# One PSUM bank moved from the recurrences to the projection, the sixth Strassen product in a bank of its own, and a set of reordered steps, in a hybrid mLSTM and SSD layer

## The chip, the core and the metric

The kernel runs on one core of one Trainium2 chip. The metric is device microseconds (us) of that core for one call, the median of several runs. Lower is better. Engines are called PE (matrix multiply), DVE (vector), ACT (scalar), POOL (GpSimd) and SP (the engine that issues every DMA of this kernel, in one in-order queue).

## What is computed

One decoder layer on 2,048 tokens of width 1,024, in float32. `reference.py`, cut to its core:

```python
h = rms_norm(x, norm_w[l])
proj = h @ w_in[l]                                   # 1024 -> 6680 columns
q, k, v, i_pre, f_pre, o_pre, z_m, z_s, xbc, dt_raw = jnp.split(proj, SPLIT_POINTS, axis=-1)
hm = mlstm_chunkwise(q, k, v, log_i, log_f)          # 4 heads, chunks of 128 tokens
hm = hm * lax.rsqrt(jnp.mean(hm * hm, -1, keepdims=True) + EPS) * mlstm_norm_w * sigmoid(o_pre) * silu(z_m)
xs, Bm, Cm = split(silu(causal_depthwise_conv(xbc)))
y = ssd_chunked(xs, softplus(dt_raw + dt_bias), A, Bm, Cm) + d_skip * xs     # 2 groups of 8 heads
y = rms_norm_per_group(y * silu(z_s)) * ssd_norm_w
x = x + concat(hm, y) @ w_out[l]
return rms_norm(x, final_norm_w)
```

## The kernel before

**Stages.** The tokens are taken as two super blocks of 1,024 (stages 0 and 1 of the program); stages 2 and 3 multiply the mixed result by the two halves of `w_out`. Every large product is one level of Strassen's scheme in a form with seven products: a job (`strassen`, L273 to 296) computes a 256 x 1,024 piece of output from seven products of 128 x 512 x 512, and there are 52 + 16 jobs. Float32 accuracy comes from splitting each operand into a high and a low half (`split`, L187; `hi` by ACT, `lo` by DVE): a product is 12 matmuls on 512 columns (L270).

**A pair's seven products** go to three PSUM banks of the pool `psp` (tag `pj`, four banks): `pa` takes L11·R11, then S2·T2, S1·T1 and S4·R22 on top; `ps` takes L12·R21; `pd` takes S3·T3, then L22·T4 on top. Each intermediate sum of `pa` is copied out by ACT (L276, L283, L289, L292) before the next product lands on it, and DVE adds `ps` or `pd` (L280, L290, L296). The order on PE interleaves two jobs: S2, S3, L11 of the next job, S1, L12 of the next job, S4, L22.

**Recurrences** are woven between these products, at most one step after each (`Weave`). `rec_head` (L661) is the mLSTM of one head: 8 chunks, `scores`, `memory`, then `gate` and `turn` some products later; `turn` multiplies the numerator by a diagonal matrix `dg` that holds the norm's factor, which transposes and scales at once (L749). `rec_group` (L774) is the SSD scan of one group: `decay` loads the rows `E` and makes the decay matrix on DVE (L797) and ACT, `tokens` transposes B and x (L812 to 816) and forms `xdt`, `cbm`, `xw` and `E` times `cbm` on DVE, `states` reads the state H (L842) and adds to it (L852, L857, L859), `outs` multiplies by E (L870), `norm` and `spread` follow three and five products later. All their PSUM tiles come from the pool `psr` (tag `rc`, four banks).

**Background work.** `next_h` (L492) normalises and splits the second super block during stage 0 and writes it to memory; its generator has 68 steps, spread over 82 products. `next_w` (L522) does the same for `w_out`. At a change of stage `refill` (L386) loads the 14 tiles of the right operand, one pair per product. `gates_mm` (L541) computes the gates' projection: it loads `wg`, splits it, and its matmuls (L562 to 564) stand on PE right behind the first job's S2 product.

Only PE's order is fixed by hand; the other engines' queues are ordered when the program is built. Each queue runs in order.

Of the kernel before, what the change touches and what calls it, by code (L numbers as in the profile page):

```python
# [69 lines left out]
def hybrid_layer(ctx, tc, x, norm_w, w_in, b_igate, b_fgate, conv_w, conv_b, dt_bias,  # L70
# [8 lines left out]
    psp = ctx.enter_context(tc.tile_pool(name="psp", bufs=4, space=PSUM))  # L79
    psr = ctx.enter_context(tc.tile_pool(name="psr", bufs=4, space=PSUM))  # L80
# [192 lines left out]
    def strassen(L, R, oa, ob, copy):  # L273
# [15 lines left out]
        nc.scalar.copy(ob[1], pa)  # L289
        nc.vector.tensor_add(ob[1], pd, ob[1])  # L290
        yield
        product(pa, L["S4"], R["R22"], False)  # L292
        copy(oa[1], pa)
# [199 lines left out]
    def next_h():  # L493

        for c in range(NCH):
# [3 lines left out]
            for i in range(2):  # L499
# [5 lines left out]
                for _ in range(4):  # L505
                    yield
# [34 lines left out]
    def gates_mm(s, R):  # L541
        wg = r2("wg", 4 * 4 * NG)
# [7 lines left out]
        wh = mk([P, 1024], "t", 1, "wgs", F32R) if s else mk([P, 6, P], "g3", 2, "wgs", F32R).rearrange("p a b -> p (a b)")  # L550
        hi, lo = wh[:, 0:16 * NG], wh[:, 16 * NG:32 * NG]
# [113 lines left out]
    def rec_head(s, h):  # L665
# [38 lines left out]
        def memory(n):  # L704
# [27 lines left out]
            dg = r5("dgm")  # L732
            nc.gpsimd.tensor_scalar_mul(dg, ident, sq)
            L["m", n] = (mx, dg)
# [8 lines left out]
        def turn(n):  # L743
            b, c = seq[n]
            mx, dg = L.pop(("m", n))
            g = L.pop(("gt", n))
            ps = rc_tile()
            for i in range(2):
                nc.tensor.matmul(ps[:, i * P:(i + 1) * P], lhsT=mx[:, i * P:(i + 1) * P], rhs=dg,  # L749
                                 start=True, stop=True)  # L750
# [25 lines left out]
    def rec_group(s, g):  # L776
# [30 lines left out]
        def tokens(n):  # L807
# [7 lines left out]
            for i in range(4):  # L815
                nc.tensor.transpose(xps[:, i * P:(i + 1) * P], t[:, 2 + i, :], ident)
            xdt = r2("xdt")
            nc.vector.tensor_tensor(xdt.rearrange(v3, e=HD), xps.rearrange(v3, e=HD),
                                    bc(G["sp"][:, c, ws], HD), op=ALU.mult)
            bt = r5("bt")  # L820
            nc.scalar.copy(bt, cps[:, P:2 * P])
            cbm = r5("cbm")
            nc.vector.tensor_mul(cbm, cps[:, 0:P], tri)
            xw = r2("xw")
            nc.vector.tensor_tensor(xw.rearrange(v3, e=HD), xps.rearrange(v3, e=HD),
                                    bc(G["dend"][:, c, hs], HD), op=ALU.mult)
# [4 lines left out]
        def states(n):  # L831
# [6 lines left out]
            y = r2("y").rearrange("p (a l) -> p a l", a=4)  # L838
            if H is not None:
# [4 lines left out]
                nc.vector.tensor_mul(y, ops.rearrange("p (a l) -> p a l", a=4), ea)  # L844
                for i in range(4):
                    nc.scalar.activation(ea[:, i, :], t[:, 2 + i, :], AF.Copy, scale=dcol[:, g, i:i + 1])
                nc.vector.tensor_add(y, y, ea)
            else:
                for i in range(4):
                    nc.scalar.activation(y[:, i, :], t[:, 2 + i, :], AF.Copy, scale=dcol[:, g, i:i + 1])  # L850
# [260 lines left out]
```

## Time and profile before

| | |
|---|---|
| median of 3 runs | 1888.11 us (1884.36 to 1892.07) |
| profiled execution, own time | 1880.11 us |
| its span | 1878.4 us |
| PE, DVE, ACT, POOL busy | 1693.1, 1299.4, 899.9, 398.6 us |
| PE granted clock, mean | 0.960 of full speed |
| DMA moved | 405.33 MB |

The profiled execution is 0.4% below the median. PE is busy for 90% of the span, so the end is set by PE's work and by the some 185 us in which it stands still. "Idle before" an instruction, with the engine and the line that it waited for, is therefore the column to read; idle time on the other engines costs nothing by itself.

### The profile page before, as it was taken

To read this page: it belongs to the slowest core of one execution; us is meant where nothing else is said; L and a number is where in the kernel's file an instruction comes from. 1 tells how busy PE (TensorE), PEld (TensorE's weight loads), DVE (VectorE), ACT (ScalarE), POOL (GpSimd) and SP (SyncE) were. 2 spreads that over 40 slices of the span, in tenths; PEclk is the share of its full clock that TensorE was granted. 3 is DMA by queue.
4 is the path that set the end of the run, shared out by engine and by line. 5 is a ranking of instruction groups with operands and counts; after the bars stand their busy time and mean duration, and the time that the engine had idled before them with its cause. 6 is when DMAs were issued, how large, how long until landed. Compare 5 with 4: busy or idle time off the path is not lost.

```text
span 1878.4 us, 25378 instructions
## 1 busy us (share of the span) xinstructions
PE 1693.1 (90%) x8200; PEld 1380.0 (73%) x8200; DVE 1299.4 (69%) x2417; ACT 899.9 (48%) x1912; POOL 398.6 (21%) x597
## 2 busy tenths in 40 slices
PE   5999999899999793998999999989979878997997
PEld 4688887788788681776788878768768667776885
DVE  7677968966657782697685886565668557863775
ACT  5345644465566551343554455555556433432443
POOL 2000303223121220032121231201112134431322
PEclk8999999999999896998999999999989989998999
DMA  5355667578778699364565758888867977578553
GB/s 149 96 166 171 192 197 214 176 244 249 233 210 233 185 308 358 98 198 134 181 181 162 240 176 271 257 285 274 270 195 256 358 264 223 185 254 336 181 161 112
DMA packets 358323, 405.33 MB, mean 216 GB/s; under 512 B 30224, under 2 KB 284432, under 8 KB 352816
## 3 DMA queue, kind: packets, MB, share of 16 engines
q1 hardware_dynamic: 358192, 403.72, 66.7%
q8 instruction: 65, 1.06, 0.2%
q14 instruction: 66, 0.54, 0.1%
HBM read 251.40 MB, written 152.24 MB: 215 GB/s over the span
## 4 chain that ended last, share of the span: by engine, by line
PE 32%; DMA 22%; DVE 12%; issue 5%; ACT 4%; SPq 3%; POOL 2%; DVEq 0%; POOLq 0%; ACTq 0%
PE pj L270 26%; DMA E<-arow 4%; DMA nmi<-mrow 3%; DVE E L797 2%; DMA we<-in_w_out 2%; DVE cd L317 2%; DMA wb<-in_w_in 1%; DMA xr<-in_x 1%; PE rc L852 1%; DMA T4l<-ws1T 1%; DMA mx<-mix 1%; DVE hql L398 1%; DMA z<-gd 1%; PE rc L870 1%; DMA ws1T<-hqh 1%
## 5 line engine op out<-in xcount | busy, mean ns | idle before, releaser
L730 POOL TENSOR_SCALAR sq<-dn,sq 128x1 f32<-128x1 f32 x64 | 50.3, 785 | 663.0 <-ACT sj L728 532.2
L270 PE MATMUL pj<-R22h,S4h 128*128 128x512 f32 x272 | 118.3, 435 | 34.7 <-ACT ob L289 19.1
L270 PE MATMUL pj<-T2h,S2h 128*128 128x512 f32 x272 | 114.9, 423 | 2.3 <-ACT T2h L441 2.3
L270 PE MATMUL pj<-T1l,S1h 128*128 128x512 f32 x272 | 107.9, 397 | 8.8 <-DMA T1l<-ws1T 7.0
L270 PE MATMUL pj<-T1h,S1h 128*128 128x512 f32 x272 | 113.1, 416 | 2.5 <-ACT ob L283 2.4
L270 PE MATMUL pj<-T4h,L22h 128*128 128x512 f32 x272 | 113.3, 416 | 1.9 <-DMA T4h<-ws1T 1.9
L270 PE MATMUL pj<-R11h,L11h 128*128 128x512 f32 x272 | 113.9, 419 | 0.0
L270 PE MATMUL pj<-R21h,L12h 128*128 128x512 f32 x272 | 112.9, 415 | 0.0
L270 PE MATMUL pj<-R22l,S4h 128*128 128x512 f32 x272 | 111.6, 410 | 0.0
L270 PE MATMUL pj<-R22h,S4l 128*128 128x512 f32 x272 | 111.6, 410 | 0.0
L270 PE MATMUL pj<-T2l,S2h 128*128 128x512 f32 x272 | 108.2, 398 | 3.2 <-DMA T2l<-ws0T 1.9
L270 PE MATMUL pj<-T3h,S3h 128*128 128x512 f32 x272 | 109.7, 403 | 0.0
L270 PE MATMUL pj<-T4l,L22h 128*128 128x512 f32 x272 | 106.9, 393 | 1.9 <-DMA T4l<-ws1T 1.9
L270 PE MATMUL pj<-T2h,S2l 128*128 128x512 f32 x272 | 108.0, 397 | 0.0
L270 PE MATMUL pj<-T1h,S1l 128*128 128x512 f32 x272 | 107.6, 396 | 0.0
L270 PE MATMUL pj<-T4h,L22l 128*128 128x512 f32 x272 | 106.9, 393 | 0.0
L270 PE MATMUL pj<-R21l,L12h 128*128 128x512 f32 x272 | 106.5, 392 | 0.0
L270 PE MATMUL pj<-R21h,L12l 128*128 128x512 f32 x272 | 106.5, 391 | 0.0
L270 PE MATMUL pj<-R11h,L11l 128*128 128x512 f32 x272 | 106.3, 391 | 0.0
L270 PE MATMUL pj<-T3l,S3h 128*128 128x512 f32 x272 | 106.1, 390 | 0.2 <-DMA T3l<-ws0T 0.2
L270 PE MATMUL pj<-T3h,S3l 128*128 128x512 f32 x272 | 106.1, 390 | 0.0
L270 PE MATMUL pj<-R11l,L11h 128*128 128x512 f32 x272 | 106.1, 390 | 0.0
(331 smaller groups left out, 4681.4 us busy)
## 6 DMA issues: line engine op xcount, KB each, us to landing
wa<-in_w_in SPq DMA_DIRECT2D x52, 512.0 KB, 5.3
s<-sum SPq DMA_DIRECT2D x52, 512.0 KB, 5.5
hd<-ob SPq DMA_DIRECT2D x32, 512.0 KB, 4.2
E<-arow SPq DMA_DIRECT2D x32, 512.0 KB, 5.4
hin<-hd SPq DMA_DIRECT2D x64, 256.0 KB, 5.6
mx<-mix SPq DMA_DIRECT2D x32, 512.0 KB, 4.4
wb<-in_w_in SPq DMA_DIRECT2D x26, 512.0 KB, 4.8
sum<-ls SPq DMA_DIRECT2D x26, 512.0 KB, 3.8
```

Source lines behind the costliest of these rows:

```text
L270: nc.tensor.matmul(ps, lhsT=l[:, k, :], rhs=r[:, k, :], start=start and k + n == 0, stop=k == 3 and n == 2, skip_group_check=True)
L317: nc.vector.scalar_tensor_tensor(dst, raw[:, q:q + SUP], cw[:, t, q:q + 1], dst, op0=ALU.mult, op1=ALU.add)
L398: nc.vector.tensor_sub(lo, src, hi.bitcast(F32))
L730: nc.gpsimd.tensor_scalar(sq, dn, DV * EPS, sq, op0=ALU.mult, op1=ALU.add)
L797: nc.vector.tensor_scalar(E[:, r, :], E[:, r, :], G["cum"][:, c, k:k + 1], 0.0, op0=ALU.subtract, op1=ALU.min)
L852: nc.tensor.matmul(sps, lhsT=bt, rhs=xw, start=True, stop=True)
L870: nc.tensor.matmul(yps[o:o + HD, (r // 2) * P:(r // 2 + 1) * P], lhsT=xdt[:, r * HD:(r + 1) * HD], rhs=E[:, r, :], start=True, stop=True, ...
```

## The change

- `psp` gets five banks, `psr` three (of eight).
- The sixth product (S4·R22) starts a bank of its own, `pe`, in place of going on top of `pa`. The running sum of `pa` after S1·T1 is copied to `oa[1]` once; DVE forms `ob[1] = pd + oa[1]` and `oa[1] = pe + oa[1]`. The ACT copy of the last sum (L292, L302) is gone; for `oz` jobs ACT applies tanh in place afterwards.
- `turn` transposes `mx` against the identity; the norm's factor is applied before that by POOL, on `mx` (128 x 256) in place of on `ident` (128 x 128).
- `tokens`: `bt` and `xw` come ahead of `xdt` and `cbm`. `states`: D·x first (ACT), H is decayed by POOL right after it was read; the product with `xw` and the addition to H form a new step `update`, one product later.
- `outs`: y squared by POOL in place of ACT.
- `next_h`: six in place of four steps between a load and its transposes, 84 steps over 76 products.
- `gates_mm` of stage 1: loaded and split one job earlier, in buffers of the tag `hq`.

```diff
-    psp = ctx.enter_context(tc.tile_pool(name="psp", bufs=4, space=PSUM))
-    psr = ctx.enter_context(tc.tile_pool(name="psr", bufs=4, space=PSUM))
+    psp = ctx.enter_context(tc.tile_pool(name="psp", bufs=5, space=PSUM))
+    psr = ctx.enter_context(tc.tile_pool(name="psr", bufs=3, space=PSUM))
...
         product(pa, L["S1"], R["T1"], False)
-        nc.scalar.copy(ob[1], pa)
-        nc.vector.tensor_add(ob[1], pd, ob[1])
+        nc.scalar.copy(oa[1], pa)
+        nc.vector.tensor_add(ob[1], pd, oa[1])
         yield
-        product(pa, L["S4"], R["R22"], False)
-        copy(oa[1], pa)
+        pe = pj_tile()
+        product(pe, L["S4"], R["R22"], True)
+        nc.vector.tensor_add(oa[1], pe, oa[1])
+        if copy is not evac_copy:
+            copy(oa[1], oa[1])
...
                 tok_norm(SUP + i * TB + c * P, None, xt)
-                for _ in range(4):
+                for _ in range(6):
                     yield
...
     def gates_mm(s, R):
-        wg = r2("wg", 4 * 4 * NG)
+        wg = mk([P, 512], "hq", 3, "wg")[:, 0:16 * NG] if s else r2("wg", 4 * 4 * NG)
...
-            dg = r5("dgm")
-            nc.gpsimd.tensor_scalar_mul(dg, ident, sq)
-            L["m", n] = (mx, dg)
+            nc.gpsimd.tensor_scalar_mul(mx, mx, sq)
+            L["m", n] = mx
...
-                nc.tensor.matmul(ps[:, i * P:(i + 1) * P], lhsT=mx[:, i * P:(i + 1) * P], rhs=dg,
-                                 start=True, stop=True)
+                nc.tensor.transpose(ps[:, i * P:(i + 1) * P], mx[:, i * P:(i + 1) * P], ident)
...
+            bt = r5("bt")
+            nc.scalar.copy(bt, cps[:, P:2 * P])
+            xw = r2("xw")
+            nc.vector.tensor_tensor(xw.rearrange(v3, e=HD), xps.rearrange(v3, e=HD),
+                                    bc(G["dend"][:, c, hs], HD), op=ALU.mult)
             xdt = r2("xdt")
...
+            for i in range(4):
+                nc.scalar.activation(y[:, i, :], t[:, 2 + i, :], AF.Copy, scale=dcol[:, g, i:i + 1])
             if H is not None:
                 ops = rc_tile()
...
-                nc.vector.tensor_mul(y, ops.rearrange("p (a l) -> p a l", a=4), ea)
...
+                nc.vector.tensor_mul(ea, ops.rearrange("p (a l) -> p a l", a=4), ea)
                 nc.vector.tensor_add(y, y, ea)
+                nc.gpsimd.tensor_tensor(H.rearrange(v3, e=HD), H.rearrange(v3, e=HD),
+                                        bc(G["cdec"][:, c, hs], HD), op=ALU.mult)
+            L["y", n] = y
+
+        def update(n):
+            bt, xdt, xw = L["a", n]
+            H = S.get("H")
             sps = rc_tile()
             nc.tensor.matmul(sps, lhsT=bt, rhs=xw, start=True, stop=True)
...
-            nc.scalar.activation(z, y, AF.Square)
+            nc.gpsimd.tensor_mul(z, y, y)
...
         for n in range(len(seq)):
             states(n)
+            yield
+            update(n)
...
     for n, jb in enumerate(jobs):
         g = jb["gen"]
+        if n + 1 < len(jobs) and jobs[n + 1]["new"] and "s" in jobs[n + 1]:
+            S["gm"] = gates_mm(jobs[n + 1]["s"], Rs[jobs[n + 1]["stage"]])
+            next(S["gm"])
...
-                total = 64 if jb["s"] else 68
+                total = 64 if jb["s"] else 84
                 for i in range(total):
-                    at(3 + i * 82 // total, bgq)
+                    at(3 + i * 76 // total, bgq)
```

**PE, the first chunk of a group, with a sixth and a seventh product** (R22h, S4h is the first matmul of the sixth, T4h, L22h that of the seventh; `pj` are projection banks, `rc` recurrence banks). Before, and then now:

```order
L812 MATMUL rc<-gin 128x128 [waits DMAHW2_49]
L813 MATMUL rc<-ident,gin 128x128
L816 MATMUL rc<-ident,gin 128x128 [waits PE_49]
...
L270 MATMUL pj<-R22h,S4h 128x512 [waits Activation_49]
...
L852 MATMUL rc<-xw,bt 128x512 [waits DVE_49,Activation_49]
L270 MATMUL pj<-T4h,L22h 128x512
...
L870 MATMUL rc<-E,xdt 64x128 [waits DVE_49,PE_49]
```

```order
L816 MATMUL rc<-gin 128x128 [waits DMAHW2_49,PE_49]
L817 MATMUL rc<-ident,gin 128x128
L820 MATMUL rc<-ident,gin 128x128 [waits PE_49]
...
L270 MATMUL pj<-R22h,S4h 128x512
...
L270 MATMUL pj<-T4h,L22h 128x512 [waits DVE_49]
...
L860 MATMUL rc<-xw,bt 128x512 [waits DVE_49,Activation_49]
L875 MATMUL rc<-E,xdt 64x128 [waits DVE_49]
```

The sixth product no longer waits for ACT (62 + 2 of the 68 did, now 11 + 2 do), and the seventh, which lands on `pd`, waits for the DVE addition that reads `pd` behind ACT's copy.

**PE, one chunk of a group** (L812 to 816, now L816 to 820: B and x transposed; L842, now L848: the state read; L852, now L860: the product with `xw`; L870, now L875: the product with E; L887 and L899, now L892 and L904: norm and spread). Before, and then now; each mark leaves out a product of 12 matmuls, and at places some other rows:

```order
L816 MATMUL rc<-ident,gin 128x128 [waits DVE_49]
...
L899 MATMUL rc<-dg,ones 128x128 [waits DVE_49,Pool_49]
L842 MATMUL rc<-gin,H 128x128 [waits DVE_49]
...
L852 MATMUL rc<-xw,bt 128x512 [waits DVE_49,Activation_49]
...
L887 MATMUL rc<-ones,q 128x1 [waits PE_49,Pool_49]
L870 MATMUL rc<-E,xdt 64x128 [waits DVE_49]
```

```order
L820 MATMUL rc<-ident,gin 128x128 [waits DVE_49]
...
L904 MATMUL rc<-dg,ones 128x128 [waits DVE_49,Pool_49]
L848 MATMUL rc<-gin,H 128x128 [waits DVE_49,PE_49]
...
L892 MATMUL rc<-ones,q 128x1 [waits DVE_49,Pool_49]
L860 MATMUL rc<-xw,bt 128x512 [waits DVE_49]
L875 MATMUL rc<-E,xdt 64x128 [waits DVE_49]
```

The product with `xw` moved behind one more product, next to that with E. With three banks the tiles of a step lie where those of the step before lay: in the built program 16 of the 30 state reads take the bank of the transposed x (free when `xw` and `xdt` are both formed), 6 that of B (free behind `cbm`), and the transposed x takes, in 25 chunks, the bank of the product with `xw` (free when DVE has added it to H). Before, no state read followed the transposes of its own chunk into their bank.

**SP, the change from stage 0 to stage 1** (R22, T4: last refills; E, ea: the first chunk's rows of the group; wg: the gates' weights). Before, and then now:

```order
L390 DMA R22l<-hsR_173 128x2048
...
L390 DMA T4l<-hsT_174 128x2048
L787 DMA gin<-gd_1_109 128x6x128
L794 DMA E<-arow_148 128x1024
L802 DMA ea<-arow_148 64x4x128 x2
L546 DMA wg<-in_w_in 128x4x8
```

```order
L549 DMA wg<-in_w_in 128x4x16
L798 DMA E<-arow_148 128x1024
...
L393 DMA R11h<-hsR_168 128x2048
...
L393 DMA R22l<-hsR_173 128x2048
...
L393 DMA T4l<-hsT_174 128x2048
```

`wg` and the first E are issued ahead of all 14 refills, where they were issued behind them.

## Rows read from the trace of the kernel before

**Rows 1.** The page, busy time of each engine, share of the span and instructions.

```profile
PE 1693.1 (90%) x8200; PEld 1380.0 (73%) x8200; DVE 1299.4 (69%) x2417; ACT 899.9 (48%) x1912; POOL 398.6 (21%) x597
```

**Rows 2.** The waits of PE over the whole run: line that waited, what it waited for, us in total, times, longest us.

```profile
PE rc L562 <- ACT wgs L552: 30.6, 1, 30.6
PE rc L852 <- DVE xw L825: 22.3, 14, 4.3
PE pj L270 <- ACT ob L289: 19.1, 10, 4.8
PE pj L270 <- ACT cbt L289: 15.5, 4, 5.5
PE rc L419 <- ACT xt L412: 9.7, 1, 9.7
PE rc L842 <- DVE aT L624: 2.0, 2, 1.3
```

**Rows 3.** PE by groups of instructions (count, busy us, mean ns of one), then two stretches of PE in order of time (start us, us, instruction). A row's time ends where the result has landed; the next start is the price.

```profile
L749 PE MATMUL rc<-dgm,mx 128*128 128x128 f32 x256 | 39.0, 275 | 2.0 <-issue 2.0
...
262.94 0.61 PE L749 MATMUL rc<-dgm,mx 128*128 128x128 f32 x4
263.30 0.48 PE L270 MATMUL pj<-T3h,S3h 128*128 128x512 f32 x1
...
274.62 0.60 PE L816 MATMUL rc<-ident,gin 128*128 128x128 f32 x4
274.98 0.47 PE L270 MATMUL pj<-R22h,S4h 128*128 128x512 f32 x1
```

**Rows 4.** The change from stage 0 to stage 1: PE and then SP in order of time (start us, us, instruction, what ended the idle time before it); R22l from issue to landing; and the window 704 to 751 us (us, then PE, weight loads, DVE, ACT, POOL busy, granted clock, DMA share, GB/s).

```profile
713.55 0.68 PE L749 MATMUL rc<-dgm,mx 128*128 128x128 f32 x4 [1.00 <-issue]
744.81 0.62 PE L562 MATMUL rc<-R11h,wgs 128*24 128x512 f32 x1 [30.58 <-ACT wgs L552]
745.23 0.63 PE L563 MATMUL rc<-R11l,wgs 128*24 128x512 f32 x1
753.03 0.40 PE L270 MATMUL pj<-T3h,S3h 128*128 128x512 f32 x1
753.26 0.39 PE L270 MATMUL pj<-T3l,S3h 128*128 128x512 f32 x1
...
718.97 2.35 SPq L390 DMA_DIRECT2D R22l<-hsR  x1
735.32 5.68 SPq L546 DMA_DIRECT2D wg<-in_w_in  x4
...
DMA to landing us min/median/max: 11.6/11.6/11.6
...
704.00:751.00 47.00, 14.73 (x54) 8.69 (x53) 9.69 (x21) 8.46 (x13) 0.00 (x0) 0.64 0.99 360
```

**Rows 5.** One late ACT copy: ACT in order of time, then the sixth product's first matmul on PE.

```profile
1251.43 0.72 ACT L533 ACTIVATE we<-we,nwo 128x512 f32<-128x512 f32 x1 [3.98 <-DMA we<-in_w_out]
1255.80 0.72 ACT L533 ACTIVATE wg<-wg,nwo 128x512 f32<-128x512 f32 x1 [1.98 <-DMA wg<-in_w_out]
1256.93 0.57 ACT L289 COPY ob<-pj 128x512 f32<-128x512 f32 x1
...
1257.56 0.80 PE L270 MATMUL pj<-R22h,S4h 128*128 128x512 f32 x1 [4.83 <-ACT ob L289]
```

**Rows 6.** SP around 620 us, in order of time.

```profile
617.35 0.37 SPq L740 DMA_DIRECT2D g<-hd  x1
626.48 0.33 SPq L321 DMA_DIRECT2D gd<-cbt  x1
626.90 0.38 SPq L403 DMA_DIRECT2D xt<-in_x  x1
```

**Rows 7.** One chunk of the first group: DVE and then PE in order of time; and the stretch of this group's recurrence (columns as in Rows 4).

```profile
339.81 2.39 DVE L797 TENSOR_SCALAR E<-E,cum 128x128 f32<-128x128 f32 x8 [0.61 <-DMA E<-arow]
342.11 0.68 DVE L818 TENSOR_TENSOR xdt<-rc,sp 128x512 f32<-128x512 f32 x1
342.91 0.68 DVE L825 TENSOR_TENSOR xw<-rc,dend 128x512 f32<-128x512 f32 x1
...
341.60 1.06 PE L842 MATMUL rc<-gin,H 128*128 128x128 f32 x8
343.73 1.10 PE L852 MATMUL rc<-xw,bt 128*128 128x512 f32 x2 [1.08 <-DVE xw L825]
...
262.00:376.00 114.00, 106.92 (x597) 86.90 (x596) 97.71 (x192) 52.79 (x105) 28.32 (x33) 1.00 0.65 201
```

**Rows 8.** Prices of operations, by groups over the whole run (count, busy us, mean ns of one, idle time before).

```profile
L296 DVE TENSOR_TENSOR ob<-pj,ob 128x512 f32<-128x512 f32 x56 | 38.4, 686 | 30.5 <-PE pj L270 30.4
L192 DVE TENSOR_TENSOR L12l<-wa,L12h 128x512 fp32r<-128x512 f32 x52 | 35.7, 686 | 8.3 <-ACT L12h L191 8.1
L192 DVE TENSOR_TENSOR L12l<-mx,L12h 128x512 fp32r<-128x512 f32 x16 | 18.6, 1160 | 0.5 <-ACT L12h L191 0.5
L733 POOL TENSOR_SCALAR dgm<-ident,sq 128x128 f32<-128x128 f32 x64 | 61.8, 966 | 6.1
L372 POOL TENSOR_TENSOR oa<-oa,xr 128x512 f32<-128x512 f32 x32 | 48.2, 1509 | 178.9 <-ACT oa L302 88.7 <-DMA xr<-in_x 49.3 <-DMA xr<-ym 28.3
L857 POOL TENSOR_TENSOR H<-H,cdec 128x512 f32<-128x512 f32 x30 | 35.7, 1189 | 96.6 <-PE rc L842 96.6
```

More of the change, by code (lines that the diff above doesn't have):

```diff
@@ L549, in gates_mm @@
         nc.vector.tensor_scalar_mul(wv[:, 3], wv[:, 0], -1.0)
-        wh = mk([P, 1024], "t", 1, "wgs", F32R) if s else mk([P, 6, P], "g3", 2, "wgs", F32R).rearrange("p a b -> p (a b)")
-        hi, lo = wh[:, 0:16 * NG], wh[:, 16 * NG:32 * NG]
+        if s:
+            hi, lo = (mk([P, 512], "hq", 3, "wgs", F32R)[:, 0:16 * NG] for _ in range(2))
+        else:
+            wh = mk([P, 6, P], "g3", 2, "wgs", F32R).rearrange("p a b -> p (a b)")
+            hi, lo = wh[:, 0:16 * NG], wh[:, 16 * NG:32 * NG]
         nc.scalar.copy(hi, wg)
@@ L744, in turn @@
             b, c = seq[n]
-            mx, dg = L.pop(("m", n))
+            mx = L.pop(("m", n))
             g = L.pop(("gt", n))
@@ L819, in tokens @@
                                     bc(G["sp"][:, c, ws], HD), op=ALU.mult)
-            bt = r5("bt")
-            nc.scalar.copy(bt, cps[:, P:2 * P])
             cbm = r5("cbm")
             nc.vector.tensor_mul(cbm, cps[:, 0:P], tri)
-            xw = r2("xw")
-            nc.vector.tensor_tensor(xw.rearrange(v3, e=HD), xps.rearrange(v3, e=HD),
-                                    bc(G["dend"][:, c, hs], HD), op=ALU.mult)
             E = L["E", n][0]
@@ L843, in states @@
                                      rhs=t[:, 1, :], start=True, stop=True)
-                nc.vector.tensor_mul(y, ops.rearrange("p (a l) -> p a l", a=4), ea)
-                for i in range(4):
-                    nc.scalar.activation(ea[:, i, :], t[:, 2 + i, :], AF.Copy, scale=dcol[:, g, i:i + 1])
+                nc.vector.tensor_mul(ea, ops.rearrange("p (a l) -> p a l", a=4), ea)
                 nc.vector.tensor_add(y, y, ea)
-            else:
-                for i in range(4):
-                    nc.scalar.activation(y[:, i, :], t[:, 2 + i, :], AF.Copy, scale=dcol[:, g, i:i + 1])
+                nc.gpsimd.tensor_tensor(H.rearrange(v3, e=HD), H.rearrange(v3, e=HD),
[4 more added lines that the diff above has]
+            H = S.get("H")
             sps = rc_tile()
@@ L856, in states @@
             else:
-                nc.gpsimd.tensor_tensor(H.rearrange(v3, e=HD), H.rearrange(v3, e=HD),
-                                        bc(G["cdec"][:, c, hs], HD), op=ALU.mult)
                 nc.vector.tensor_add(H, H, sps)
-            L["y", n] = y
         def outs(n):
@@ L914, in rec_group @@
             states(n)
+            yield
+            update(n)
             if s == 0 and n + 1 == len(seq):
                 nc.sync.dma_start(hdd[g], S["H"])
-            yield
             outs(n)
@@ L1032, in hybrid_layer @@
         g = jb["gen"]
+        if n + 1 < len(jobs) and jobs[n + 1]["new"] and "s" in jobs[n + 1]:
+            S["gm"] = gates_mm(jobs[n + 1]["s"], Rs[jobs[n + 1]["stage"]])
+            next(S["gm"])
         if jb["new"] and "s" in jb:
             s = jb["s"]
-            gm = gates_mm(s, Rs[s]) if s else gm0
+            gm = S.pop("gm") if s else gm0
             if s:
-                next(gm)
                 at(1, gm)
```

## The prediction

> **What bounds the kernel now.** I read the page's table of engines first: PE is busy 90% of the span and no other engine more than 69% [rows 1], so the end is set by PE's own work plus the 1878.4 − 1693.1 = 185 us in which it stands still. Next I read PE's waits, to see which of the 185 us have a named cause that the diff touches [rows 2]: 30.6 us in one wait for the gates' weights; 22.3 us in 14 waits of the product with `xw`; 19.1 + 15.5 = 34.6 us in 14 waits of a sixth product for ACT's copy of the bank it lands on; 9.7 us in one wait for `xt`. That is 97 us; the rest of the idle time lies in small pieces that no part of the change is aimed at. Last I read the stretches around these waits in order of time, for what made each one late and what stands next behind it.
>
> **The change part by part**, against the profiled execution's own 1880.11 us.
>
> *Transposes in `turn`.* The multiplications by `dg` make 256 records for 128 calls, two passes each [rows 3]. Four records cost PE 0.36 us (262.94 to 263.30). Transposes against `ident` make one record per call: four calls show four records and 0.36 us (274.62 to 274.98). 128 records go, at 0.36 / 4 = 0.09, or 0.11 counting the fill of each group: 11.5 to 14.1 us. PE is the bound in the head phases, so I take **−13**. In return POOL scales 256 columns in place of 128. The old scaling took 966 ns [rows 8], so 64 times between nothing and 0.97 us are added, on an engine busy 21%; the step runs some products ahead of `turn`, which covers it.
>
> *The gates' weights.* At 714.2 us PE stops for 30.58 us until `wgs` is there [rows 4]. SP gets to `wg` only at 735.32, behind all refills. In the new order `wg` and the first E are issued ahead of them, and the wait ends. What is late next is the last refill that the gates' products read: R22l is issued at 718.97 and takes 11.6 to land, so it is there at 730.6. From 714.2 PE has 24 gate matmuls at 0.23 (the spacing 753.03 to 753.26), 5.5 us, and two products of 12, 5.4 us, ahead of it; at 725.1 it stops again, for some 5.5. Gain 30.6 − 5.5 = 25.1. After the long stop the granted clock of the window is 0.64 [rows 4] and the first matmuls stand 0.42 apart (744.81 to 745.23) in place of 0.23; some 13 of these would no longer be so, 2.5 us. I take **−26**; ends −18 (the refills collide with the earlier E) and −33 (no new stop).
>
> *The sixth product.* It no longer lands on the bank that ACT must copy. But the seventh lands on `pd`, which DVE reads (L290) only after that same copy. In the late case shown, ACT stands behind two instructions that wait for DMA (3.98 and 1.98 us), copies at 1256.93, and PE starts 4.83 late [rows 5]. The ACT queue is not cleared by the change; the copy comes as late as before. PE gains one product of cover, 12 × 0.227 = 2.72, less the DVE addition of 0.686 [rows 8], and about 0.06 for the hand-over: at most 1.97 per event. With 14 events of 34.6 us in all, of which the mean is 2.5 and the longest 5.5, cutting each by the smaller of itself and 1.97 gives about 20; I take **−19**. Ends: −34.6 (all of it) and −8 (the copies come later still). DVE gains 68 additions of 0.686, 46.6 us, on an engine at 69%; ACT loses 52 copies of 0.57 [rows 5], 30 us, and 32 squares.
>
> *`xt`.* SP issues a load of `g` at 617.35 and then stands until a store of `gd` is ready at 626.48; the load of `xt` is issued behind it, at 626.90 [rows 6], and PE waits 9.7 [rows 2]. In the new order the last `xt` stands ahead of that store. I take **−8**; ends 0 (another store is in its way) and −9.7.
>
> *Group phases.* The product with `xw` moves one product (2.72 us) later than the state read, so its own waits, 22.3 us, should go. But the pool has three banks. In 16 of 30 chunks the state read itself now waits for `xw` and `xdt`. In the chunk shown [rows 7] DVE forms the two at 342.11 and 342.91, so the read could start at 343.7 in place of 341.60, 2.1 us late. If all 16 lie like that, they cost 33.6; if only as often as the product with `xw` waited (14 of 30), 15.7. Less 22.3, this is +11 or −7. The single buffer of E closes a loop from chunk to chunk (E is loaded when the chunk before has been multiplied with it, and DVE stands 0.61 for it at 339.81), which hands delays on, so I take the upper half, **+8**. Ends: −22 (no new wait) and 30 × 2.1 − 22 = +41. POOL's squaring of y is not shown; nearest are 512 columns at 1.19 and 1.51 us [rows 8], 32 times, some 43 us, on the idle engine; the norm follows three products later, which covers it.
>
> *Three banks elsewhere.* In the head phases and the token transposes a tile is now taken sooner after its last use; counted in the built program, uses with under two us of PE work in between go from 16 to 35. The nearest row is a state read that waits, 2.0 us in 2 waits [rows 2]. 19 × 1.0, if some two in five wait, is **+8**; ends 0 and 19 × 1.3 = +25.
>
> Sum: −13 − 26 − 19 − 8 + 8 + 8 = −50, so 1830 for an execution like the profiled one. That lay 8.0 us below the median of the runs; the forecast for the median is **1838**.
>
> **A rule weighed against the trace.** DVE's rows show that an operation with both inputs in SBUF takes 686 ns from `wa`, but 1160 ns from `mx`, in the stages in which POOL runs its own additions of 1509 ns [rows 8]: DVE loses part of POOL's time, some 0.47 of 1.5 us. The Trainium skill says more (page "SBUF — State Buffer", section "SBUF: two separate sides"): DVE with two SBUF inputs and GpSimd reading SBUF share a port pair as an exclusive lock, and the loser blocks for the whole instruction. By the row the squares moved to POOL cost DVE 8 × 0.47 = 4 us per group phase, inside its slack; by the rule 8 × 1.35 = 11, which is rival B.
>
> **Rivals.** *A, slower: three recurrence banks tie PE to DVE at every step of a chunk.* Each of the 30 chunks then waits three times: the transposes for the addition to H, the state read for `xdt`, the product with E for what it takes over. It decides from the point at which the mean of 90 waits exceeds what the other terms save, 66 + 22 of the `xw` waits already counted as gone: from (66 − 8)/90 = 0.65 us each the change loses. At 0.9 us it is 1888 − 66 + 8 + 81 = 1911. For it: the mean wait at the product with `xw` is 22.3/14 = 1.6 [rows 2], and DVE is busy 97.7 of 114 us in the first group's stretch [rows 7]. Against it: most chunks have DVE ahead, since only 14 of 30 waited at all. Chance 0.08.
>
> *B, DVE becomes the bound in the group phases.* If POOL's squares block DVE for all their time, its work there is 97.7 + 4 × 0.686 + 10.8 = 111 of 114 us, and with the waits that any chain has each of the four phases would grow by some 5 us: 1838 + 20 = 1858. For it the slow rows, against it that they show a third of that. Chance 0.12.
>
> *C, the waits vanish without heirs.* No new stop behind the gates, the sixth product's 34.6 and the 22.3 of `xw` all go: −13 − 33 − 34.6 − 22.3 − 9.7 = −113 and +8 for banks: 1888 − 105 = 1783. For it: ACT has fewer copies, so it may run less late. Against it the chain behind `pd`. Chance 0.13.
>
> *D, the change doesn't do what it says.* For the sixth product and the gates the orders exclude it. What remains is SP: the queue is written anew, and a load behind a store that waits, as in [rows 6], could cost one 30 to 50 us stop and bring it back to 1880. Chance 0.05.
>
> **How the numbers follow.** My forecast has 0.62: 1838, by its own ends from about 1812 to 1868 (the ends of single terms do not all fall on one side). With B (0.12), C (0.13), A (0.08) and D (0.05), a range that leaves out no more than 2 in 10 reaches from 1783, C's full size, to 1884, just above D: it leaves out A and the outer parts of C and D, some 0.17. A measurement of this kernel tells about 0.5%, 9.4 us, from no change: "same" is 1878.7 to 1897.5. Faster: the forecast, B, C and half of D are 0.89, less 0.08 for the upper tails of the forecast and of B: 0.81. Same: these tails and the rest of D, 0.10. Slower: A, and 0.01 of D's upper part, 0.09.
>
> **Signs.** Right: the rows of `turn` fall to 128 records and PE's busy time by some 14 us; no sixth product waits for ACT, while a seventh now waits for DVE's L290; the stop of 30 us at 714 is gone and a stop of some 5 us stands before R22's gate products; the waits at L852 are gone, others stand at the state read (L848) and the transposes (L816, L820); `xt` no longer waits; DVE is busy some 45 us longer, POOL 45 to 100. Wrong: waits of PE in the group phases that sum to more than 60 us (A), DVE's own rows longer by the time of POOL's (B), PE's idle time under 90 us (C), a new stop of over 20 us behind a transfer (D).

## The result, and the profile after

| | before | changed |
|---|---|---|
| median | 1888.12 us (1884.36 to 1892.07, 4 runs) | 1859.42 us (1853.58 to 1864.46, 4 runs) |
| ratio to before | | 0.985, 95% interval 0.981 to 0.989 |
| profiled execution, own time | 1880.11 us | 1856.56 us |

The change makes the kernel 28.7 us faster; forecast was 50. The page's first line, against [rows 1]:

```profile
PE 1684.8 (91%) x8072; PEld 1359.3 (73%) x8072; DVE 1341.2 (72%) x2485; ACT 858.9 (46%) x1828; POOL 450.9 (24%) x629
```

PE's busy time fell by 8.3 us and its idle time from 185 to 170. DVE's busy time rose by 42, to 72% of the span. PE is still the busiest, but what it waits for has changed: summed over the rows of its waits, ACT ended 86.7 us of them before and 21.0 now, DVE 57.1 before and 106.5 now. Next come PE's waits, against [rows 2] (line, what it waited for, us in total, times, longest):

```profile
PE rc L848 <- DVE xdt L827: 28.5, 14, 3.9
...
PE rc L816 <- DMA gin<-gd: 12.9, 1, 12.9
...
PE pj L270 <- ACT ca L276: 7.1, 1, 7.1
...
PE pj L270 <- DVE ob L290: 4.5, 4, 2.5
...
PE pj L270 <- DVE cbt L290: 3.6, 2, 3.0
...
PE rc L569 <- DMA R22l<-hsR: 1.9, 1, 1.9
```

The wait for `wgs`, all of a sixth product's waits for ACT and that for `xt` of L412 are gone; what a seventh product waits for DVE is 4.5 + 3.6 = 8.1 us. New are the state read's 28.5 and, at the change of stage, a short wait for R22l. The heads' new waits are best seen in the groups of PE's instructions (count, busy, mean ns | idle before, what ended it):

```profile
L754 PE MATMUL rc<-ident,mx 128*128 128x128 f32 x128 | 25.3, 279 | 29.3 <-DVE dn L729 16.0 <-ACT vt L707 5.0 <-DVE C L726 3.7
...
L721 PE MATMUL rc<-vt,kw 128*128 128x258 f32 x128 | 40.0, 395 | 8.8 <-DVE g L755 6.5 <-ACT mx L735 2.2
L717 PE MATMUL rc<-vt,st 128*128 128x258 f32 x128 | 38.8, 385 | 4.2 <-ACT vt L707 2.0 <-ACT qg L514 1.8 <-ACT qe L514 0.2
```

The rows of `memory` before, which L721 and L717 are now:

```profile
L711 PE MATMUL rc<-vt,st 128*128 128x258 f32 x128 | 39.0, 387 | 2.1 <-ACT vt L701 2.1
...
L715 PE MATMUL rc<-vt,kw 128*128 128x258 f32 x128 | 38.8, 385 | 0.0
```

`turn` (L754) stood idle 2.0 us before [rows 3] and stands 29.3 now; with L721 and L717 it is 42.3, where it was 4.1.

Since the order of the products on PE is the same in both programs, the two traces can also be laid side by side product by product, by the start of each of the 476. The time between fixed products, in us, for these and for kernels told of below:

| stretch (products) | before | changed | gates_only | banks_back | swap_only | update_back | banks_update_back |
|---|---|---|---|---|---|---|---|
| change of stage (182 to 189) | 67.6 | 39.0 | 43.7 | 45.8 | 63.1 | 39.9 | 41.7 |
| four group phases | 599.3 | 610.1 | 601.2 | 585.7 | 607.7 | 607.4 | 606.5 |
| four head phases | 926.8 | 919.6 | 923.0 | 910.7 | 937.9 | 929.4 | 921.0 |
| start and output stages | 247.2 | 246.3 | 244.7 | 245.4 | 249.2 | 242.8 | 243.2 |

The change of stage gave 28.6 us. The groups lost 10.8, and the heads, in which the transposes and the sixth product should have given over 30, gave 7.2. There is one trace of each kernel, and executions of one kernel lie some 10 us apart (1853.58 to 1864.46 for the change), so a few us between two columns can't be told from that spread; a reading here needs a row of waits beside it.

### The profile page after: what moved, and what is told of

The parts are those of the page before. It is cut to its first block, busy times and chain, and to the rows that moved or that the text cites. A ratio compares the mean times of both kernels' runs of the same rounds, so it can differ in the third digit from the quotient of the medians.

```text
span 1854.8 us, 25098 instructions
## 1 busy us (share of the span) xinstructions
PE 1684.8 (91%) x8072; PEld 1359.3 (73%) x8072; DVE 1341.2 (72%) x2485; ACT 858.9 (46%) x1828; POOL 450.9 (24%) x629
## 4 chain that ended last, share of the span: by engine, by line
PE 50%; DMA 23%; DVE 15%; issue 5%; ACT 4%; SPq 2%; POOL 1%; DVEq 0%; ACTq 0%; POOLq 0%
PE pj L270 40%; DMA E<-arow 4%; DVE E L801 2%; DMA ws1T<-hql 2%; PE rc L848 1%; DMA mx<-mix 1%; DMA nmi<-mrow 1%; DMA we<-in_w_out 1%; PE rc L875 1%; DMA ws0R<-hqh 1%; DMA g<-hd 1%; PE rc L860 1%; PE rc L721 1%; DMA T4l<-ws1T 1%; DMA z<-gd 1%
## 5 line engine op out<-in xcount | busy, mean ns | idle before, releaser
L736 POOL TENSOR_SCALAR sq<-dn,sq 128x1 f32<-128x1 f32 x64 | 43.5, 679 | 626.5 <-ACT sj L734 461.6
L270 PE MATMUL pj<-R22h,S4h 128*128 128x512 f32 x272 | 111.9, 411 | 0.0
L270 PE MATMUL pj<-R22l,S4h 128*128 128x512 f32 x272 | 107.0, 393 | 0.0
L270 PE MATMUL pj<-R22h,S4l 128*128 128x512 f32 x272 | 107.0, 393 | 0.0
L270 PE MATMUL pj<-R11h,L11l 128*128 128x512 f32 x272 | 106.5, 391 | 0.0
```

Of the source, the lines that this page charges most:

```text
L270: nc.tensor.matmul(ps, lhsT=l[:, k, :], rhs=r[:, k, :], start=start and k + n == 0, stop=k == 3 and n == 2, skip_group_check=True)
L736: nc.gpsimd.tensor_scalar(sq, dn, DV * EPS, sq, op0=ALU.mult, op1=ALU.add)
```

## The experiments

Each was timed in five rounds against the kernel before, whose median lay between 1884.26 and 1889.22 us in these sessions. Ratios are to that kernel in the same session; where two experiments come from different sessions, the ratios compare them better than the medians. Edits are against the changed kernel where nothing else is said; `...` marks left-out lines.

**1. gates_only: the kernel before with one piece.**

```diff
-        wg = r2("wg", 4 * 4 * NG)
+        wg = mk([P, 512], "hq", 3, "wg")[:, 0:16 * NG] if s else r2("wg", 4 * 4 * NG)
...
+            S["gm"] = gates_mm(jobs[n + 1]["s"], Rs[jobs[n + 1]["stage"]])
+            next(S["gm"])
...
```

> The kernel before with one piece of the change alone: the gates' weights of stage 1 loaded and split one job earlier, in buffers of the tag hq. Theory (nearly the whole gain of the change comes from this piece, and what the others win is given back by the three recurrence banks): the step of 28.6 us at the change of stage, seen product by product between the two traces, comes alone; 1860, and a profile with no wait of 30 us at 714. Rival (each piece gives its own share): some 1870, because the refills and the early loads collide without the shifted background work.

Measured: 1856.57 us, ratio 0.985 (0.981 to 0.988), as the theory had it. This piece alone gives as much as the whole change; all others together come out at nothing.

**2. banks_back: four and four banks, the sixth product on `pa`, all else as changed.**

```diff
-    psp = ctx.enter_context(tc.tile_pool(name="psp", bufs=5, space=PSUM))
-    psr = ctx.enter_context(tc.tile_pool(name="psr", bufs=3, space=PSUM))
+    psp = ctx.enter_context(tc.tile_pool(name="psp", bufs=4, space=PSUM))
+    psr = ctx.enter_context(tc.tile_pool(name="psr", bufs=4, space=PSUM))
...
-        pe = pj_tile()
-        product(pe, L["S4"], R["R22"], True)
-        nc.vector.tensor_add(oa[1], pe, oa[1])
...
+        product(pa, L["S4"], R["R22"], False)
+        copy(oa[1], pa)
```

> The changed kernel with four projection and four recurrence banks again, and the sixth product on top of pa with ACT's copy, as before; everything else as in the change. Theory (the third recurrence bank costs what the sixth product's own bank saves, or more): waits of turn and memory (28.8 + 11.6 us of gaps) mostly vanish, the sixth product's waits of some 27 us net return; 1845 to 1855. Rival (the late ACT copy is one stop, which only changes the line at which it shows): no net move, 1855 to 1865. Rival (the bank pays): 1875 or more.

Measured: 1829.31 us (1826.97 to 1834.99), ratio 0.970 (0.967 to 0.974): 30 us faster than the change, more than the theory said, and the fastest version of this study. PE's waits:

```profile
PE pj L270 <- ACT ob L289: 24.6, 12, 6.2
...
PE pj L270 <- ACT cbt L289: 10.9, 5, 4.7
...
PE pj L270 <- ACT ca L276: 9.3, 1, 9.3
...
PE rc L751 <- POOL mx L735: 2.0, 1, 2.0
```

The sixth product waits 24.6 + 10.9 = 35.5 us for ACT, as before. But the waits of `turn` fall from 29.3 to 2.0, those at the state read vanish, and in the table the groups are 24.4 and the heads 8.9 us shorter than with the change. The edit puts back two things at once: the fourth recurrence bank, and the way the sixth product is copied out, which takes 68 additions off DVE. Experiment 6 parts the two, in the order of the kernel before; in the changed order they were not parted.

**3. diag_back: the diagonal matrix in `turn` again.**

```diff
-            nc.gpsimd.tensor_scalar_mul(mx, mx, sq)
+            nc.gpsimd.tensor_scalar_mul(dg, ident, sq)
...
-                nc.tensor.transpose(ps[:, i * P:(i + 1) * P], mx[:, i * P:(i + 1) * P], ident)
+                nc.tensor.matmul(ps[:, i * P:(i + 1) * P], lhsT=mx[:, i * P:(i + 1) * P], rhs=dg,
...
```

> The changed kernel with the diagonal matrix in turn again (POOL scales ident 128 x 128, PE multiplies mx by it: 256 records), three recurrence banks kept. Theory (turn waits for its bank, not for POOL's longer scaling): turn's gaps of 28.8 us stay, PE's busy time rises by 14; 1870 to 1874. Rival (turn waits because POOL scales 256 columns in place of 128): the gaps fall by over half, 1855 or less.

Measured: 1873.93 us, ratio 0.993 (0.990 to 0.996): 14.5 us slower than the change, as the theory had it. Not so its reason in full: the idle time of `turn` (L755 here) did not stay but fell from 29.3 to 18.8 us, while that of L721, which often takes the bank of `turn`, rose from 8.8 to 17.2:

```profile
PE rc L721 <- DVE g L757: 13.3, 8, 3.4
...
PE rc L755 <- DVE C L726: 7.2, 4, 3.5
...
PE rc L755 <- DVE dn L729: 6.5, 4, 3.4
```

**4. w_lead: two steps between the loads of `w_out` and their scaling.**

```diff
                         nc.sync.dma_start(u, w_out[r * P:(r + 1) * P, b * TB:(b + 1) * TB])
-                        nc.scalar.activation(u, u, AF.Copy, scale=nwo[:, r:r + 1])
+                        todo.append((u, r))
+                yield
                 yield
+                for u, r in todo:
+                    nc.scalar.activation(u, u, AF.Copy, scale=nwo[:, r:r + 1])
+                yield
```

> The changed kernel with two more steps between the loads of w_out and ACT's scaling of them (80 steps in place of 64 over the same 76 products), so that ACT no longer stands in front of a load that has not landed. Theory (the waits at turn in stage 1's head phases come from ACT and DVE held up behind these loads, and only show at turn because its bank is the next thing wanted): the gaps of turn between 1158 and 1397 us, some 23 us, fall to under 8; 1838 to 1848. Rival (turn waits for the pace of the recurrence on three banks): within 3 us of the change, 1856 to 1862.

Measured: 1870.26 us, ratio 0.992 (0.989 to 0.995): slower by 11, and the gaps of `turn` stay. The edit did not do what it was for. ACT's waits for these loads, first in the changed kernel, then here:

```profile
ACT we L536 <- DMA we<-in_w_out: 10.4, 5, 7.1
...
ACT wg L536 <- DMA wg<-in_w_out: 3.2, 2, 1.7
```

```profile
ACT we L541 <- DMA we<-in_w_out: 16.8, 7, 7.1
...
ACT wg L541 <- DMA wg<-in_w_out: 12.0, 6, 3.5
```

They grew from 13.6 to 28.8 us: the ACT queue is ordered when the program is built, and a later step in the source did not put the scaling behind the landing. So the run neither proves nor refutes the theory. Of the 15 us between the two traces, 10.5 lie between products 280 and 364 (335.7 us where the change took 325.2), the head phases beside which these loads run. That goes the theory's way, but it is no proof.

**5. swap_only: the kernel before with the exchange of banks and the sixth product's bank alone** (the inverse of edit 2 on the kernel before).

> The kernel before with the exchange of banks alone: five projection banks, three for recurrences, and the sixth product in its own bank; no other move. Theory (the exchange loses, since the run with the banks put back is 30 us faster than the change): 1910 to 1925, sixth products no longer wait for ACT, and waits of over 60 us appear in the recurrences. Rival (the exchange loses only together with the later update of the state): 1880 to 1895. Rival of the prediction's sum (-19 + 8 + some of the 8): 1880 or less.

Measured: 1899.55 us, ratio 1.007 (1.004 to 1.010): slower by 13, between the theory (1910 or more) and its rival (1895 or less), and against the sign that the prediction's terms gave this part. The rows of `turn` and `memory`, and what the seventh product waits for:

```profile
L752 PE MATMUL rc<-dgm,mx 128*128 128x128 f32 x256 | 41.0, 283 | 24.4 <-ACT vt L704 11.6 <-DVE dn L726 5.9 <-issue 4.4
L718 PE MATMUL rc<-vt,kw 128*128 128x258 f32 x128 | 39.7, 392 | 14.6 <-DVE g L754 11.2 <-ACT mx L732 3.4
L714 PE MATMUL rc<-vt,st 128*128 128x258 f32 x128 | 38.6, 383 | 1.5 <-DVE C L721 1.2 <-ACT vt L704 0.3
```

```profile
PE pj L270 <- DVE ob L290: 5.0, 6, 1.6
...
PE pj L270 <- DVE cbt L290: 3.8, 1, 3.8
```

No sixth product waits for ACT, but the heads are 11.1 us longer than before, and `turn` and `memory` stand idle 40.5 us.

**6. rec3_only: the kernel before with three recurrence banks and one bank unused.**

```diff
-    psr = ctx.enter_context(tc.tile_pool(name="psr", bufs=4, space=PSUM))
+    psr = ctx.enter_context(tc.tile_pool(name="psr", bufs=3, space=PSUM))
```

> The kernel before with three recurrence banks and one bank left unused; the sixth product still on top of pa. With the exchange alone it splits the loss into the bank taken from the recurrences and the bank given to the sixth product. Theory (the two add up): the exchange's time plus some 20 us, 1930 to 1945. Rival (one late ACT causes both waits, and a stop at either covers the other): about the time of the exchange alone, within 8 us.

Measured: 1895.76 us, ratio 1.005 (1.003 to 1.007). The rival was right. Taking a bank away costs 9 us, and using it for the sixth product brings nothing on top: 1899.55 with it, 1895.76 without. With three banks the sixth product already waits less:

```profile
PE pj L270 <- ACT cbt L289: 14.4, 3, 5.3
...
PE pj L270 <- ACT ob L289: 8.6, 3, 4.4
```

```profile
L749 PE MATMUL rc<-dgm,mx 128*128 128x128 f32 x256 | 40.2, 280 | 11.8 <-DVE dn L723 4.9 <-issue 3.9 <-DVE C L720 1.8
...
L715 PE MATMUL rc<-vt,kw 128*128 128x258 f32 x128 | 39.6, 391 | 14.6 <-DVE g L751 14.6
```

14.4 + 8.6 = 23.0 us in place of 34.6 [rows 2], while `turn` and `memory` (L749, L715; L711 stands 0.0) go from 4.1 to 26.4 us. The two places share one delay, as the rival had it: where PE stops for it at one, it stops less at the other.

**7 and 8. no_w, banks_no_w: ACT's exponential `w` left out**, on the changed kernel and on banks_back.

```diff
-            nc.scalar.activation(w, nmi[:, 0, P - 1:P], AF.Exp, bias=G["u"][:, c, h:h + 1])
+            w = E[:, P - 1:P]
-            nc.vector.scalar_tensor_tensor(qp, t[:, 0, :], QS, nmi[:, 1, :], op0=ALU.mult, op1=ALU.mult)
+            nc.vector.tensor_mul(qp, t[:, 0, :], nmi[:, 1, :])
```

> The changed kernel without ACT's separate exponential w in scores: the last column of E serves as the factor, the scale moves from q to the state, so ACT has no instruction that needs only the row nmi (38 waits of 85.7 us in all, in front of that load) in its queue. Three recurrence banks kept. Theory (ACT held up by that load delays kw, vt, mx and the projection's copies, and the three banks pass the delay to PE): the gaps of turn and memory, 31.1 + 14.4, fall by 20 or more; 1835 to 1845. Rival (the next instruction that needs the row, the exponential of E, stands in the same place): 1853 to 1862.

> The run with the banks put back, and in addition without w as above. Theory: the sixth product's waits for ACT, 35.5 us in 17, fall by a third or more; 1812 to 1820. Rival (E's exponential waits in w's place): 1826 to 1833.

Measured: 1861.33 us, ratio 0.986 (0.983 to 0.989), and 1834.50 us, ratio 0.972 (0.969 to 0.975). Neither moved beyond the spread of its partner, and `turn` waits as long as in the change:

```profile
PE rc L753 <- DVE dn L728: 16.0, 5, 4.1
```

The theory fell: ACT's own wait for that row does not decide. The rival was near with the times, but not by its reason. ACT's wait for E, first in the changed kernel, then in no_w:

```profile
ACT E L691 <- DVE E L689: 8.6, 11, 2.9
```

```profile
ACT E L691 <- DVE E L689: 17.8, 15, 3.5
```

It grew by 9 us, where 85.7 us of waits for `w` went away. So most of ACT's waiting in front of that row was no part of what holds PE up; what does was not found here.

**9. banks_update_back: banks_back with the state's update joined to its read, `xw` formed last.**

```diff
             states(n)
-            yield
-            update(n)
             if s == 0 and n + 1 == len(seq):
                 nc.sync.dma_start(hdd[g], S["H"])
+            yield
```

The body of `update` stands at the end of `states`.

> The run with the banks put back (four and four), and with the state's update joined to its read again and xw formed last, as before; POOL's squares, the early decay of H and all else as in the change. Theory (with four banks the later update takes away the waits for xw, some 31 us of gaps at the state steps, and the three banks alone turn this gain into waits at the state read): the groups lengthen by 12 to 18 us; 1841 to 1848. Rival (the groups gain through the squares on POOL and the early decay of H): 1829 to 1834.

Measured: 1854.57 us, ratio 0.983 (0.981 to 0.985): 25 us slower than banks_back, more than the theory said, and 20.8 longer in the groups. The waits for `xw` are back:

```profile
PE rc L853 <- DVE xw L826: 36.4, 15, 5.4
```

**10. update_back: the same edit with the change's five and three banks.**

> The changed kernel, five and three banks, with the state's update joined to its read again and xw formed last, as before; all else as in the change. With four recurrence banks the same edit cost 25 us. Theory (with three banks the later update only moves its waits from the product with xw to the state read, so that its gain needs the fourth bank): 1857 to 1865. Rival (the later update is worth as much with three banks, and the exchange of banks costs its 30 us apart from it): 1880 to 1888.

Measured: 1868.05 us, ratio 0.993 (0.990 to 0.996): 9 us slower than the change by the medians, 15 by the two ratios (0.993 and 0.985), between theory and rival. In the traces the groups take 607.4 us against the change's 610.1, so there the later update shows no gain with three banks. The waits only change their line:

```profile
PE rc L848 <- DVE cbm L827: 23.5, 15, 3.5
```

The heads, which the edit doesn't touch, are 9.8 us longer; `turn` and `memory` stand idle 50.0 us there against 42.3, and why is open. So the rows of the groups speak for the theory, the whole time leaves the later update a worth of 9 to 15 us, and this is not settled.

**11. banks_xt_back: banks_back with the old steps of `next_h`.**

```diff
-                for _ in range(6):
+                for _ in range(4):
-                total = 64 if jb["s"] else 84
-                    at(3 + i * 76 // total, bgq)
+                total = 64 if jb["s"] else 68
+                    at(3 + i * 82 // total, bgq)
```

> The run with the banks put back, and next_h with four steps and 68 over 82 products again. The prediction's term: PE waits 9.7 us for xt again, 1837 or more. Theory (the stop of 9.7 us had moved to ACT's copy into ca, which waits for that buffer's store, 9.3 us): the one wait comes, the other goes; 1828 to 1832.

Measured: 1850.64 us, ratio 0.978 (0.975 to 0.980): 21 us slower by the medians, 14 by the ratios. In the stage of `xt` both kernels take the same time: product 182 comes 1.3 us later here, counted from the first product, with 10.0 us of wait for `xt` and none for `ca`. So the forecast's time came and the theory's reason did: the one wait comes, the other goes. The rest lies behind the change of stage, 13 us in stage 1 and 7 in the last group phase. The first lines of the pages, banks_back and then this run:

```profile
PE 1676.2 (92%) x8072; PEld 1354.5 (74%) x8072; DVE 1305.1 (71%) x2417; ACT 878.8 (48%) x1880; POOL 451.8 (25%) x629
```

```profile
PE 1689.1 (91%) x8072; PEld 1362.8 (74%) x8072; DVE 1305.2 (71%) x2417; ACT 878.8 (48%) x1880; POOL 448.2 (24%) x629
```

Of the 22.0 us between the two traces 12.9 are busy time of PE for the same 8072 instructions, at a mean granted clock of 0.963 against 0.969; the other 9 are idle time. The edit also spaces the steps of `next_w` (82 products in place of 76), which neither the forecast nor the theory had counted; how much of the difference that is was not separated.

**12. banks_copy_pd: banks_back with ACT's copy taken from `pd`.**

```diff
         product(pd, L["S3"], R["T3"], True)
+        nc.scalar.copy(ob[1], pd)
         yield
         product(pa, L["S1"], R["T1"], False)
-        nc.scalar.copy(ob[1], pa)
-        nc.vector.tensor_add(ob[1], pd, ob[1])
+        nc.vector.tensor_add(ob[1], pa, ob[1])
```

> The run with the banks put back, and in each pair ACT copies pd right behind the third product, two products earlier, and DVE adds pa to that; no more instructions than before. The sixth product then waits for DVE's addition and no longer for a copy by ACT that came in behind ACT's waits. Theory (late ACT, not the missing bank, made the sixth product wait): its 35.5 us in 17 waits fall below 12; 1803 to 1812. Rival (DVE is as late as ACT, or the delay moves on to the next bank): 1825 to 1832.

Measured: 1847.47 us, ratio 0.977 (0.975 to 0.980): slower by 18.

```profile
PE pj L270 <- DVE ob L290: 19.7, 13, 6.5
...
PE pj L270 <- DVE cbt L290: 12.9, 3, 9.3
```

The sixth product now waits 19.7 + 12.9 = 32.6 us for DVE, where it waited 35.5 for ACT. Late ACT alone was not the cause: DVE is as late, as the rival said. Its additions (L290) stood idle for PE alone, 14.5 us, and never for ACT's copy, so they came late in DVE's own queue; what holds that queue was not traced. Where the 18 us come from (13 by the ratios) was not separated; the heads are 13 us longer.

## Why the prediction was right, and where its steps failed

The sign and the range held, but by one term; the others were wrong in both directions and cancelled. That the total fell into the range is, for those terms, luck.

*Transposes, −13: right.* Two passes became one: L754 has 128 records and 25.3 us where L749 had 256 and 39.0 [rows 3], and undoing it cost 14.5. PE's busy time in all fell by 8.3 only, where the signs had some 14; its other rows grew by 5 us, and why is open.

*The gates' weights, −26: right*, 28.6 between the traces and 31 alone. The stops behind it are 1.08 and 1.95 us, not 5.5:

```profile
734.18 0.39 PE L568 MATMUL rc<-R22h,wgs 128*24 128x512 f32 x1 [1.08 <-DMA R22h<-hsR]
736.52 0.41 PE L569 MATMUL rc<-R22l,wgs 128*24 128x512 f32 x1 [1.95 <-DMA R22l<-hsR]
```

To compare the times, count from product 182, which starts at 703.15 us before and 8 us later, at 711.16, now. PE gets to the stop 21.9 us after it (734.18 − 1.08 = 733.1), as the step had it (725.1). What shortened the stop is the refill: R22l is there some 25.4 us after product 182, where the step had 27.4. In the window 704 to 751 us the granted clock is 0.96 where it was 0.64 [rows 4]:

```profile
704.00:751.00 47.00, 41.93 (x183) 28.87 (x182) 18.23 (x43) 14.75 (x29) 1.90 (x7) 0.96 1.02 380
```

*The sixth product, −19: the wait went, the gain did not.* 34.6 us of waits became 8.1 at the seventh, so 26.5 left this place, more than forecast. But rec3_only and swap_only show that with three recurrence banks the extra bank, with its 68 additions on DVE, is worth nothing (1895.76 against 1899.55). The delay shows at the next bank that PE wants. PE's idle time in us, at `turn` and `memory` and at the product that waits for the evacuation:

| | before | banks_back | rec3_only | swap_only | changed |
|---|---|---|---|---|---|
| recurrence banks | 4 | 4 | 3 | 3 | 3 |
| `turn` and `memory` | 4.1 | 3.4 | 26.4 | 40.5 | 42.3 |
| sixth product (seventh, where the sixth has its own bank) | 34.6 | 35.5 | 23.0 | 8.8 | 8.1 |
| sum | 38.7 | 38.9 | 49.4 | 49.3 | 50.4 |

The sum hardly depends on where the sixth product goes: its own bank moves 14 us from the one row to the other. It depends on the fourth recurrence bank, which is worth some 11 us of these waits, near the 9 us that rec3_only lost. In the changed order the groups add to it: the state read stands 33.8 us with three banks and 1.2 with four (banks_back).

*Three banks elsewhere, +8 with an upper end of 25: the step that failed.* L754, L721 and L717 stand idle 42.3 us, where L749, L715 and L711 stood 4.1 us. I had counted the banks taken again within two us of PE work. By PE's busy time in the trace of the changed kernel, only 4.7 of the 42.3 us stand at such reuses; most stand at reuses a little longer than that. With the banks of the built program, 15 of the 64 turns now take the bank of L721 after 2.6 to 3.0 us of PE's busy time and wait 16.6 us, 17 take that of the scores after 3.9 to 4.3 and wait 5.9, and in 21 cases L721 takes that of a turn within 4.2 and waits 6.5. Before, no turn took a bank after less than 6.2 us. One such wait, first ACT, then DVE, then PE, in order of time (start us, us, instruction, idle time before it):

```profile
1269.98 0.30 ACT L693 ACTIVATE w<-nmi,u 128x1 f32<-128x1 f32 x1 [3.07 <-DMA nmi<-mrow]
...
1272.34 0.72 ACT L536 ACTIVATE we<-we,nwo 128x512 f32<-128x512 f32 x1 [1.55 <-DMA we<-in_w_out]
```

```profile
1273.74 0.69 DVE L401 TENSOR_TENSOR hql<-we,hqh 128x512 fp32r<-128x512 f32 x1 [2.23 <-ACT hqh L399]
...
1275.75 0.48 DVE L726 SCALAR_TENSOR_TENSOR C<-C,nmi,rc 128x258 f32<-128x258 f32 x1
1276.14 0.15 DVE L729 COPY dn<-rc 128x1 f32<-128x1 f32 x1
```

```profile
1267.83 0.70 PE L721 MATMUL rc<-vt,kw 128*128 128x258 f32 x2
...
1276.37 0.54 PE L754 MATMUL rc<-ident,mx 128*128 128x128 f32 x2 [5.10 <-DVE dn L729]
```

ACT stands 3.07 and 1.55 us for loads; DVE's casts stand for ACT; the state's addition C, which releases the bank that this `turn` takes, comes at 1275.75, over seven us after its product (L721 at 1267.83), and `turn` starts 5.10 late. (The row names `dn`, which DVE ends just behind C; in the built program PE waits for C.) In the kernel before such lateness fell on a sixth product [rows 5] and had cover at `turn`. So the sum should not have had −19 and +8 as two terms: they are one delay that moves, and the lost bank adds to it.

*Group phases, +8: near (10.8 between the traces), and the mechanism held.* All of the 28.5 us that the state read waits for `xdt` stand at the 16 reads that take the bank of the transposed x, 14 of which wait, 2.0 each; the step had 2.1 each, for all 16 or for half of them. The waits forecast at the transposes (L820) did not come. A chunk of the group of [rows 7], one with the wait:

```profile
334.59 0.68 DVE L824 TENSOR_TENSOR xw<-rc,dend 128x512 f32<-128x512 f32 x1
335.19 0.68 DVE L827 TENSOR_TENSOR xdt<-rc,sp 128x512 f32<-128x512 f32 x1
```

```profile
336.02 1.13 PE L848 MATMUL rc<-gin,H 128*128 128x128 f32 x8 [1.73 <-DVE xdt L827]
...
339.87 1.10 PE L860 MATMUL rc<-xw,bt 128*128 128x512 f32 x2
```

`xw` now comes first, and the product with it (339.87) does not wait; the state read does, 1.73 us, for `xdt`. What I did not see is how much the step gives with four banks: 25 us, with 20.8 in the groups and 36.4 us of waits for `xw` back (banks_back against banks_update_back). How much of that three banks take away is less sure (experiment 10). One word on the section on the change: a state read that follows the transposes of its own chunk into their bank was there before too, once, and waited 0.9 us for `cbm`.

*`xt`, −8: its wait went, the gain did not.* ACT's copy into `ca` stood for that buffer's store, and PE 7.06 us for the copy, near the same place (PE had gone on at 634.86 us before, and goes on at 639.11 now):

```profile
638.48 0.59 ACT L276 COPY ca<-pj 128x512 f32<-128x512 f32 x1 [3.34 <-DMA gd<-ca]
```

```profile
639.11 0.79 PE L270 MATMUL pj<-T2h,S2h 128*128 128x512 f32 x1 [7.06 <-ACT ca L276]
```

Saved are 2.6 us. It is the end at which the term was put to nothing, another store in the way.

*The rivals.* A was not the whole, but its mechanism was there, in the heads more than in the groups: the state read, the transposes and the product with E stand under 40 us for DVE, where A's sign was over 60, and the exchange alone does make the kernel before slower (1.007). B did not come: DVE's busy time is 1341.2, under the 1299.4 + 46.6 = 1346 that its instructions would take at their old durations, so POOL's squares (32 at 1117 ns) did not make it the bound. The Trainium skill's rule of the exclusive lock (page "SBUF — State Buffer", section "SBUF: two separate sides") would, by an estimate from the row of the squares, have asked for 32 × 1.1 = 35 us more at most. Where the two meet, the trace agrees with it; here POOL's square, then a DVE row that takes 0.69 us elsewhere:

```profile
329.18 1.36 POOL L883 TENSOR_TENSOR z<-y 128x512 f32<-128x512 f32 x1 [2.03 <-issue]
```

```profile
329.68 1.41 DVE L204 TENSOR_TENSOR ls<-ls,wa 128x512 f32<-128x512 f32 x1
```

But of the 42 DVE instructions that overlap a square only nine are longer than usual, by 3.9 us in all. C and D did not come either: PE's idle time is 170 us, not under 90, and its longest wait is one of 12.9 us for `gin`, which was 11.9 before.

## What to carry to other kernels

A buffer taken from a chain that had slack is not free because no wait shows there: count for every reuse how much work lies between the last writer and the next, and compare it with the lateness that the stalls elsewhere show (here up to 5.5 us), not with a threshold of one's own. Where in-order queues run late, a stall is a delay that can be moved; removing its place was worth nothing here, since the delay had no cover at the next place. Time the parts of a bundle apart: here one part gave 31 us, one lost 30, and the rest gave 27. The worth of parts doesn't add up either: of the rest, two parts taken back singly cost 25 and 21 us.

## What the runs showed of the hardware

Where DVE and POOL met on SBUF operands, a DVE instruction of 0.69 us took 1.41 beside a POOL instruction of 1.36; over the run that came to 3.9 us. Of this program the runs showed that parts which an edit does not touch move: the heads by 9.8 us in update_back, the four group phases by 17 us in sum in banks_xt_back (602.8 against 585.7 with the same code). Over that whole run more than half of the difference is PE's own busy time, at a lower granted clock; the rest was not explained.
